# Encoder block on one core: fewer weight planes in front of attention, a third probability buffer, squares on ScalarE alone, first columns over seven buffers

## The chip, the cores and the metric

The kernel runs on one core of a Trainium2 chip. The engines of a core work on their own instruction queues, each in its own order, and wait for one another by semaphores: TensorE (PE, matrix products into PSUM banks), VectorE (DVE), ScalarE (ACT), GpSimd (POOL), and SyncE (SP), which here issues nearly all DMA transfers. The metric is the device time of one execution in microseconds (us); a time is a median of several executions.

## The reference

An encoder block on 1024 tokens of width 1024, batch 1, depth 1:

```python
h = layer_norm(x, ln0_g, ln0_b)
proj = h @ w_in + b_in                       # qa ka va | qb kb vb | ga gb
y_na  = neighbourhood_attention(qa, ka, va, na_rpb) @ w_branch_na     # 8 heads, 16x64 grid
y_swa = windowed_gqa_with_sink(rot(qb), rot(kb), vb, swa_sink) @ w_branch_swa  # 8 heads, window 128
mixed = sigmoid(ga) * y_na + sigmoid(gb) * y_swa
h = layer_norm(2**0.25 * h + mixed @ w_out + b_out, ln1_g, ln1_b)
u = square(relu(h @ w_ff1 + b_ff1))
h = layer_norm(2**0.25 * h + u @ w_ff2 + b_ff2, ln2_g, ln2_b)
```

Everything is float32. The kernel keeps that accuracy by splitting each factor of a product into a high and a low 16-bit plane (or a high and a low rounded 32-bit part in attention) and adding three products: high by high, high by low, low by high.

## The kernel before, in words

**Stages.** First layer norm and transposition of the tokens, with the first two gate chunks' products (0 to about 48 us of the profile); projections in front of attention (to 92); 16 attention heads with the other projections woven between (to about 400); the rest of the gates by a Strassen-like scheme of seven products (to about 500); branch products, output projection and second layer norm; the two feed-forward layers, seven products again, to the end.

**First columns.** `ln0_turn(half, k)` takes transposed column k (128 features) of one half (512 tokens) out of PSUM. ScalarE writes the affine result `t` in float32 (L384), then the high plane is made by ScalarE (L383, for k in `HI_ACT`) or DVE (L386), and the low plane (L387) by GpSimd if k is in `LO_ON[half]`, else by DVE. Three of four groups of `t` are stored to DRAM (`hq_d`, L391), and the buffer of `t` is free again only when that store has landed. `t` borrows buffers that attention uses later: `vt` and `x2` (one each), `pl` (two) and `pt` (three). `PRE_AT` says at which column iteration i a preparation step of chunk 0 or 1 is issued.

**Chunks.** The projection weights come in 24 chunks of 1024x128 (`fills`), numbered j from 0: 0 and 1 are key and value of the windowed attention, 2 its first queries, 3 to 8 more queries and gates, 9 on the neighbourhood attention. Each is prepared in five steps (`Chunk.to`): (1) sum of squares, on ScalarE (L213) or, from `ON_DVE` on, on DVE (L210); (2) a total over partitions by two small PE matmuls (L193); (3) a scale from it, DVE (L199) and GpSimd (L200); (4) the high plane on ScalarE (L252); (5) the low plane on DVE (L254). Raw weights lie in a ring of three places, so chunk j's load waits until chunk j-3's low plane is made. The planes lie in a ring of three pair buffers (`wpair`), except for chunks 3 to 8, which have places of their own (`KEPT`).

**Order of the work.** The order on every engine is written out by hand. A generator (`fill`) issues one chunk matmul (L418) at a time; chunk j's 48 matmuls are numbers 48j to 48j+47. `pump(n)` issues n of them, and lowers the counters of all deferred work (`later`) by n; `flush` issues, in the order of the list, what has come due. `plan` puts the load and the preparation steps of all chunks on that list, ahead of everything else, with due counts relative to 48j: in the change below, `t` holds the counts of steps 1, 2-3, 4 and 5. In front of attention the loop issues 4 matmuls and flushes, 188 in all (`N_PRE`). The work that follows a projection half (24 matmuls) is deferred too: eviction at once (L595, L500 and others), then for rotated queries and keys the shuffle (DVE, L603) and three GpSimd passes (L605 to L607) 4 later, the high parts (ScalarE casts, L651, or L630 and L631 for the key) 22 after that, the low parts (DVE, L656, or L636) 8 later still.

**Attention.** `steps(s, n, ...)` handles a quarter of a head: scores of piece s+2 by PE (L753, L754) with bias and row maximum on DVE (L755), some of the n chunk matmuls, an early flush (preparation steps 1, 4 and 5 are issued only here), `part_l(s + 1)`: low plane of the probabilities on DVE (L786) and the transposing DMA from `pl` to `pt` (L789), `part_e(s + 2)`: exponentials (ScalarE, L774) and their scaled high plane into `pl` (L777), another flush, more chunk matmuls, `part_c(s - 1)`: probabilities by values on PE (L861), and a last flush, in which totals are issued. n is 12 in the first eight heads and 18 in the last eight. An output bank is drained by ScalarE (L867) and, deferred by 14, by DVE (L870). For the neighbourhood heads, L534 evicts a query-key projection, L537 to L539 cast its high parts (ScalarE) and L544 and L545 make its low parts (DVE).

**The gates behind attention.** `g_mm(p, i)` is product i of gate pair p (12 matmuls of four 128-row blocks, L1138), `g_after` takes it out (ScalarE, L1200, or DVE, L1203) and stores it, `g_sums` forms the next weight sums on DVE (L1107), `g_hi` and `g_lo` their planes (L1123, L1127). `g_do` is the product and, for products 1, 6, 5 and 4, its `g_after`. Product 4 accumulates on the bank that product 7's `g_after` reads.

Of the kernel before, what the change touches and what calls it, by code (L numbers as in the profile page):

```python
# [12 lines left out]
F16 = mybir.dt.float16  # L13
# [3 lines left out]
P = 128  # L17
D = 1024
S = 1024
NK = D // P  # L20
# [38 lines left out]
W_TOP = 8192.0  # L59
Q_MIN = 1e-30  # L60
C_LAG = 1
LO_ON = (2, 3, 4, 5), (1, 3, 5)
RS = 3, 3.5, 4.5, 5.5
HI_AT = 1
PRE_AT = {8: (0, 1), 10: (0, 3), 16: (0, 4), 18: (0, 5), 20: (1, 1)}
KEPT = {3: 'whi0', 4: 'wlo0', 5: 'whi1', 6: 'wlo1', 7: 'raw', 8: 'raw'}
ON_DVE = 12
PREP = 5, 6, 7, 8, 8, 9, 10, 12, 13, 14, 15, 16
HI_ACT = (0, 2, 3, 4, 5), ()
ST0=2  # L70
# [22 lines left out]
def encoder_block(ctx, tc, x, w_in, w_br, w_out, w_ff1, w_ff2, par, rows, rpbp,  # L93
# [131 lines left out]
    class Chunk:  # L225
        def __init__(self, kept=None, on_dve=False):
            i = len(chunks) % 3
            self.raw, self.n, self.on_dve = wraw[i], 0, on_dve
            if kept:
                self.pair = wp.tile([P, 2, 8, P], F16, tag=kept, name="wpair", bufs=2 if kept == "raw" else 1)  # L230
            else:
                self.pair = wpair[n_pair[0] % 3]
                n_pair[0] += 1
            chunks.append(self)

# [140 lines left out]
    def ln0_turn(half, k):  # L376
        cs = slice(half * 512, (half + 1) * 512)
        ps = ln_ps[half, k]
        tag = ("vt", "pl", "x2", "pt")[k % 4]
        t = ap.tile([P, 512], F32, tag=tag, name="t", bufs=dict(pl=2, pt=3).get(tag, 1))  # L380
        aff = dict(bias=g0s[:, 8 + k:9 + k], scale=g0s[:, k:k + 1])
        if k in HI_ACT[half]:
            ACT.activation(hT[:, 0, k, cs], ps, AF.Identity, **aff)  # L383
        ACT.activation(t, ps, AF.Identity, **aff)  # L384
        if k not in HI_ACT[half]:
            DVE.tensor_copy(hT[:, 0, k, cs], t)  # L386
        (POOL if k in LO_ON[half] else DVE).tensor_tensor(out=hT[:, 1, k, cs], in0=t, in1=hT[:, 0, k, cs],  # L387
                                               op=ALU.subtract)
        q = f"A{half + 1}{k // 4 + 1}"
        if q in hq_d:  # L390
            nc.sync.dma_start(hq_d[q][:, k % 4], t)  # L391
# [300 lines left out]
    def plan():  # L692

        def to(j, n):
            return lambda: got[j].to(n)
        ev = []
        for j in range(1, len(todo)):
            u = 48 * j
            t = (u - 84, u - 60, u - 40, u - 20) if j > 8 else \
                [24 * j - 32 + x for x in (0, 14, 38, 44)]  # L700
            if j > 8:
                ev.extend((u - 140 + 8 * x, 0, (j, x)) for x in range(4))
            elif j > 2:
                ev.append((max(24 * (j - 3) + 14, 2), 0, (j, None)))
            ev.extend((x, n, j) for x, n in zip(t, (1, 3, 4, 5)))
        for x, n, j in sorted(ev, key=lambda e: e[0]):
            if n == 0:
                defer(x, lambda j=j: fetch(*j))
            else:
                defer(x, to(j, n), pe=n == 3, only=n != 3)  # L710
# [53 lines left out]
    def part_e(s):  # L764
# [7 lines left out]
        for i, (at, n, c0) in enumerate(tiles):  # L772
            p = e[:, at:at + n]
            ACT.activation(p, p, AF.Exp, bias=nm[:, i:i + 1], scale=-1.0,  # L774
                           accum_out=sums_l[o_chunk][:, hh, 2 * t + i:2 * t + i + 1])
        pl = ap.tile([P, 1536], F16, tag="pl", name="pl")
        ACT.activation(pl[:, 0:n_all], e[:, 0:n_all], AF.Copy, bias=0.0, scale=P_SCALE)  # L777
        hd.pairs[t] = e, tiles, n_all, pl

# [130 lines left out]
    with tc.manual_schedule(engines=MANUAL):  # L910
# [324 lines left out]
        def g_do(p, i):  # L1235
            g_mm(p, i)
            if i in (1, 6, 5, 4):
                g_after(p, i)
# [64 lines left out]
        g_do(3, 3)  # L1303
        g_after(3, 3)
        g_lo(3, 4)
        g_sums(1, 6)
        g_hi(1, 6)
        g_do(2, 7)
        g_lo(1, 6)
        g_after(2, 7)  # L1310
        g_sums(0, 6)
        g_hi(0, 6)
        g_do(3, 7)
# [1113 lines left out]
```

## Time and profile before

| | |
|---|---|
| median of 3 runs | 1264.71 us (1263.72 to 1265.9) |
| profiled execution, its own time | 1266.1 us |
| its span, first to last instruction | 1264.3 us |
| mean granted TensorE clock | 0.990 |
| busy share: PE, DVE, ACT, POOL | 97%, 77%, 66%, 27% |
| DMA | 216.83 MB, mean 172 GB/s |

The profile comes from one execution, recorded by the hardware. A row of an order of time is: start, length, engine, line, operation, what it writes and reads, how many instructions are merged in it (x), and in brackets the engine's idle time before it and what ended that. PEld is TensorE's weight load, which overlaps its products. "hT" is the name of one large tile that also holds the raw weights, the weight pairs and small scales of the chunks.

### The profile page before, as it was taken

What the parts mean: (1) busy time and instruction counts of PE and PEld (TensorE: products, weight loads), DVE (VectorE), ACT (ScalarE), POOL (GpSimd) and SP (SyncE); (2) the same over time, 40 slices, a digit from 0 to 9 for tenths busy, and PEclk for the clock granted to TensorE, in tenths of its full rate; (3) what the DMA queues carried; (4) which work ended last, traced back from release to release, by engine and by line L of the source; (5) the groups of instructions that cost most, each with busy time, mean ns of one, the idle gap of its engine ahead of it and who ended that gap; (6) DMA issues with size and microseconds to landing.
All of it is one profiled execution on the core that took longest, in us unless ns stands there. A gap on an engine that the chain in (4) does not pass through costs nothing.

```text
span 1264.3 us, 16965 instructions
## 1 busy us (share of the span) xinstructions
PE 1226.1 (97%) x6024; PEld 673.7 (53%) x6024; DVE 974.5 (77%) x1396; ACT 829.5 (66%) x1329; POOL 346.6 (27%) x352
## 2 busy tenths in 40 slices
PE   7988999899999999999999999999999999999997
PEld 5545665555555446888884444444444444444443
DVE  6667998798797976444778988787767778898888
ACT  7576789787776645432657877877877646434457
POOL 5462231343341001334731013323300001201207
PEclk9998999899999999999999999999999999999999
DMA  8462668677754425555343267766637635363333
GB/s 320 167 201 73 150 160 186 128 165 155 164 139 126 161 83 183 193 174 216 124 160 117 103 199 248 230 237 221 222 132 259 231 133 226 125 254 129 125 108 134
DMA packets 177877, 216.83 MB, mean 172 GB/s; under 512 B 111744, under 2 KB 125312, under 8 KB 171136
## 3 DMA queue, kind: packets, MB, share of 16 engines
q1 hardware_dynamic: 176816, 214.89, 53.8%
q8 instruction: 47, 0.77, 0.3%
q10 hardware_dynamic: 976, 0.87, 0.2%
q14 instruction: 38, 0.31, 0.1%
HBM read 130.69 MB, written 59.33 MB: 150 GB/s over the span
## 4 chain that ended last, share of the span: by engine, by line
PE 72%; DVE 11%; ACT 7%; DMA 4%; issue 4%; POOL 2%; SPq 0%; POOLq 0%; ACTq 0%; DVEq 0%
PE ps_mm L418 12%; PE ps_o L1660 6%; PE ps_t L1660 6%; PE ps_s L2132 6%; PE ps_mm L2132 6%; PE ps_mm L1660 5%; PE ps_t L2132 5%; PE ps_o L2132 5%; PE ps_s L1660 2%; PE ps_o L861 2%; DMA pt<-pl 1%; PE ps_t L410 1%; PE ps_o L410 1%; PE ps_t L409 1%; PE ps_o L409 1%
## 5 line engine op out<-in xcount | busy, mean ns | idle before, releaser
L418 PE MATMUL ps_mm<-hT 128*128 128x512 f16 x960 | 229.8, 383 | 9.5 <-DVE hT L254 4.4
L1660 PEld LDWEIGHTS <-tw 128*128 128x128 f16 x1248 | 122.1, 99 | 145.1 <-issue 1.7
L2132 PEld LDWEIGHTS <-hS 128*128 128x128 f16 x1008 | 98.6, 98 | 118.2
L418 PEld LDWEIGHTS <-hT 128*128 128x128 f16 x960 | 90.9, 100 | 109.4 <-issue 15.9
L774 ACT ACTIVATE ss<-ss,sk 128x384 f32<-128x384 f32 (+1 forms) x128 | 73.9, 579 | 38.0 <-DVE sk L755 37.8
L1660 PE MATMUL ps_t<-hS,tw 128*128 128x512 f16 x384 | 87.9, 379 | 0.0
L1415 POOL TENSOR_TENSOR mx<-sg 128x512 f32<-128x512 f32 x16 | 32.5, 2033 | 142.2 <-DVE sg L1414 142.2
L786 DVE SCALAR_TENSOR_TENSOR pl<-ss,pl 128x640 f16<-128x640 f32 (+1 forms) x64 | 69.0, 1078 | 2.3 <-ACT pl L777 1.8
L418 PE MATMUL ps_mm<-hT,wpair 128*128 128x512 f16 x288 | 70.4, 385 | 0.0
L1850 DVE TENSOR_TENSOR usl<-usl 128x512 f32<-128x512 f32 x64 | 51.4, 803 | 23.6 <-ACT usl L1778 23.4
L1581 POOL TENSOR_TENSOR c<-c 128x2 f32<-128x2 f32 x16 | 15.6, 978 | 194.0 <-DVE c L1580 194.0
L2152 POOL TENSOR_TENSOR acc<-acc,rst 128x512 f32<-128x512 f32 x16 | 30.2, 1886 | 124.0 <-DMA rst<-xr_d 116.1
L777 ACT ACTIVATE pl<-ss 128x640 f16<-128x640 f32 (+1 forms) x64 | 50.6, 790 | 19.1 <-DMA pt<-pl 17.6
L200 POOL TENSOR_TENSOR hT<-hT 128x2 f32<-128x2 f32 x30 | 26.6, 889 | 128.7 <-DVE hT L199 128.7
L1138 PEld LDWEIGHTS <-hT 128*128 128x128 f16 x336 | 33.3, 99 | 43.1 <-issue 5.3
L1965 DVE SCALAR_TENSOR_TENSOR hS<-stg,c,hS 128x2048 f16<-128x2048 f32 x21 | 49.9, 2378 | 7.6 <-ACT hS L1962 7.6
L1587 DVE SCALAR_TENSOR_TENSOR tw<-raw,c,tw 128x512 f16<-128x512 f32 x60 | 51.8, 864 | 4.5 <-ACT tw L1584 4.2
L2132 PEld LDWEIGHTS <-hA 128*128 128x128 f16 x336 | 32.9, 98 | 39.6
L861 PE MATMUL ps_o<-pt,vv 128*128 128x256 f16 (+1 forms) x448 | 49.7, 251 | 3.7 <-DVE oT L870 3.3
L861 PEld LDWEIGHTS <-vv 128*128 128x128 f16 x448 | 35.7, 98 | 21.1 <-DVE oT L870 4.2
L1660 PE MATMUL ps_o<-hS,tw 128*128 128x512 f16 x192 | 44.0, 379 | 0.0
L1584 ACT ACTIVATE tw<-raw,c 128x512 f16<-128x512 f32 x60 | 41.7, 709 | 2.8 <-DVE raw L1625 2.8
(398 smaller groups left out, 3072.0 us busy)
## 6 DMA issues: line engine op xcount, KB each, us to landing
us_d<-usl SPq DMA_DIRECT2D x112, 256.0 KB, 3.0
stg<-us_d SPq DMA_DIRECT2D x28, 1024.0 KB, 4.8
raw<-in_w_ff SPq DMA_DIRECT2D x24, 512.0 KB, 5.4
sg<-sg_d SPq DMA_DIRECT2D x32, 256.0 KB, 3.6
hA<-in_w_ff SPq DMA_DIRECT2D x8, 1024.0 KB, 7.4
hS<-in_w_ff SPq DMA_DIRECT2D x8, 1024.0 KB, 7.8
hT<-in_w_in SPq DMA_DIRECT2D x60, 128.0 KB, 2.6
hT<-in_w_in SPq DMA_DIRECT2D x11, 512.0 KB, 4.4
```

Source lines behind the costliest of these rows:

```text
L418: PE.matmul(ps, a[:, k, :], act(b, k), start=(k == 0 and i == 0), stop=(k == NK - 1 and i == 2))
L774: ACT.activation(p, p, AF.Exp, bias=nm[:, i:i + 1], scale=-1.0, accum_out=sums_l[o_chunk][:, hh, 2 * t + i:2 * t + i + 1])
L777: ACT.activation(pl[:, 0:n_all], e[:, 0:n_all], AF.Copy, bias=0.0, scale=P_SCALE)
L786: DVE.scalar_tensor_tensor(out=pl[:, n:2 * n], in0=e[:, 0:n], scalar=P_SCALE, in1=pl[:, 0:n], op0=ALU.mult, op1=ALU.subtract)
L861: PE.matmul(o, vs, move(part), start=(m == 0 and part == 0), stop=(m == len(runs) - 1 and part == 1))
L1138: PE.matmul(ps, w[:, a, k, :], act[:, b, k, :], start=(first and k == 0 and m == 0), stop=(k == 3 and m == 2), skip_group_check=True)
L1584: ACT.activation(hi_lo(slot, 0), src, AF.Copy, bias=0.0, scale=w_scale(p))
L1587: DVE.scalar_tensor_tensor(out=hi_lo(slot, 1), in0=src, scalar=w_scale(p), in1=hi_lo(slot, 0), op0=ALU.mult, op1=ALU.subtract)
L1660: PE.matmul(ps, ww, act[:, part, k, :], start=(first and k == 0 and m == 0), stop=(k == 3 and m == 2), skip_group_check=True)
L1850: DVE.tensor_tensor(out=out, in0=a, in1=b, op=op)
L1965: DVE.scalar_tensor_tensor(out=slot[:, :, 1, :], in0=src, scalar=scale, in1=slot[:, :, 0, :], op0=ALU.mult, op1=ALU.subtract)
L2132: PE.matmul(ps, st[:, a, part, j * P:(j + 1) * P], w[:, a, wpart, :], start=(first and a == 0 and m == 0), stop=(a == 3 and m == 2), skip_ ...
```

## The change

Six edits:

- `LO_ON`: column 5 of the first half leaves GpSimd; its low plane is made by DVE. `PRE_AT`: chunk 0's total and scale are issued at i = 12 in place of 10. `ln0_turn`: `t` goes round seven buffers in place of the four names in turn.
- `ON_DVE = 99`: the squares of chunks 12 to 23 go from DVE to ScalarE.
- `Chunk`: from the sixth chunk without a place of its own (that is chunk 9) on, the planes take two pair buffers in turn, not three.
- `part_e`: every third `pl` lies in the third pair buffer's place, so that there are three places for probabilities.
- `plan`: chunks 1 to 6 are due every 20 counts in place of 24, chunks 7 and 8 only behind the start of attention (200 to 304); for chunks 9 on, squares are due at u-96 (was u-84), totals at u-72 (u-60), high planes at u-44 (u-40), low planes at u-28 (u-20), loads 10 earlier, with u = 48j.
- the gates: product 7 of pair 2 and its `g_after` come ahead of the sums and the high plane for product 6 of pair 1.

```diff
-LO_ON = (2, 3, 4, 5), (1, 3, 5)
+LO_ON = (2, 3, 4), (1, 3, 5)
-PRE_AT = {8: (0, 1), 10: (0, 3), 16: (0, 4), 18: (0, 5), 20: (1, 1)}
+PRE_AT = {8: (0, 1), 12: (0, 3), 16: (0, 4), 18: (0, 5), 20: (1, 1)}
-ON_DVE = 12
+ON_DVE = 99
@@ class Chunk
-                self.pair = wpair[n_pair[0] % 3]
+                self.pair = wpair[n_pair[0] % 3 if n_pair[0] < 5 else n_pair[0] % 2]
                 n_pair[0] += 1
@@ ln0_turn
-        tag = ("vt", "pl", "x2", "pt")[k % 4]
+        tag = ("vt", "pl", "x2", "pt", "pl", "pt", "pt")[(half * NK + k) % 7]
@@ plan
             u = 48 * j
-            t = (u - 84, u - 60, u - 40, u - 20) if j > 8 else \
-                [24 * j - 32 + x for x in (0, 14, 38, 44)]
+            t = (u - 96, u - 72, u - 44, u - 28) if j > 8 else \
+                [200 + 40 * (j - 7) + x for x in (0, 24, 44, 64)] if j > 6 else \
+                [20 * j - 24 + x for x in (0, 14, 30, 34)]
             if j > 8:
-                ev.extend((u - 140 + 8 * x, 0, (j, x)) for x in range(4))
+                ev.extend((u - 150 + 8 * x, 0, (j, x)) for x in range(4))
             elif j > 2:
-                ev.append((max(24 * (j - 3) + 14, 2), 0, (j, None)))
+                ev.append((max(20 * (j - 3) + 12, 2) + (30 if j > 6 else 0), 0, (j, None)))
             ev.extend((x, n, j) for x, n in zip(t, (1, 3, 4, 5)))
@@ part_e
-        pl = ap.tile([P, 1536], F16, tag="pl", name="pl")
+        pl = ext[:, 10240:11776] if s % 3 == 0 else ap.tile([P, 1536], F16, tag="pl", name="pl")
@@ the gates
         g_lo(3, 4)
+        g_do(2, 7)
+        g_after(2, 7)
         g_sums(1, 6)
         g_hi(1, 6)
-        g_do(2, 7)
         g_lo(1, 6)
-        g_after(2, 7)
         g_sums(0, 6)
         g_hi(0, 6)
         g_do(3, 7)
```

## The prediction

> **What bounds the kernel now.** I read the page first, then TensorE's list of waits, then the order of time of each engine around each wait.
>
> ```profile
> span 1264.3 us, 16965 instructions
> PE 1226.1 (97%) x6024; PEld 673.7 (53%) x6024; DVE 974.5 (77%) x1396; ACT 829.5 (66%) x1329; POOL 346.6 (27%) x352
> PE ps_s L753 <- DVE q L656: 6.7, 1, 6.7
> PE ps_mm L418 <- DVE hT L254: 4.4, 5, 1.9
> PE ps_o L861 <- DVE oT L870: 3.3, 1, 3.3
> PE ps_o L1138 <- DVE go L1203: 2.4, 1, 2.4
> ```
>
> TensorE (PE) is busy 97% of the span, so it sets the end, and what can be won lies in the 38 us in which it isn't. The list (total, times, longest) says where: 6.7 us in one wait for a split query (L656) as attention starts, 4.4 us for late low weight planes (L254), 3.3 us for an output bank to be drained (L870), 2.4 us in the gate products (L1203). A wait can also cost clock. First three waits in order of time (start, length, and in brackets the idle time before), then stretches of time with their length, the busy time of PE, PEld, DVE, ACT and POOL, and PE's granted clock.
>
> ```profile
> 262.14 1.47 PE L418 MATMUL ps_mm<-hT 128*128 128x512 f16 x6 [1.33 <-DVE hT L254]
> 306.45 1.89 PE L418 MATMUL ps_mm<-hT 128*128 128x512 f16 x6 [1.92 <-DVE hT L254]
> 351.03 1.47 PE L418 MATMUL ps_mm<-hT 128*128 128x512 f16 x6 [0.63 <-DVE hT L254]
> ```
>
> ```profile
> 95.73:102.56 6.83, 3.97 (x11) 2.01 (x12) 4.50 (x7) 2.44 (x6) 3.23 (x2) 0.50 0.00 0
> 225.44:232.27 6.83, 6.25 (x22) 3.46 (x23) 5.24 (x11) 5.36 (x13) 1.67 (x2) 0.50 0.80 186
> 262.99:266.40 3.41, 3.41 (x18) 1.90 (x17) 3.38 (x9) 1.62 (x3) 1.86 (x4) 1.00 0.13 30
> 307.36:310.77 3.41, 3.41 (x11) 1.91 (x10) 3.38 (x9) 1.45 (x3) 1.56 (x3) 0.50 0.26 59
> ```
>
> Behind the waits that end at 98.6, 226.0 and 306.5 the clock is 0.5 for 6.8, 6.8 and 3.4 us. Half of what PE worked there is lost: 2.0, 3.1 and 1.7 us. Behind the wait of 1.33 us, which ends at 262.1, the clock stays whole. So a wait of 1.3 us costs itself, and one of 1.9 us cost 3.6. [...]
>
> **First columns, and a squares' total two columns later.**
>
> ```profile
> 22.40 0.78 ACT L384 ACTIVATE t<-ps_s,hT 128x512 f32<-128x512 f32 x1 [1.56 <-DMA hq_dA<-t]
> 22.02 0.27 POOL L349 TENSOR_SCALAR mv<-mv 128x1 f32<-128x1 f32 x1
> 31.46 0.38 PE L193 MATMUL ps_t<-hT 128*128 128x2 f32 x2 [0.71 <-ACT hT L213]
> ```
>
> ScalarE (ACT) waits 1.56 us for a store to free "vt" in column 4; with seven buffers that column has a fresh one. Only part comes through: the normalisation behind it needs GpSimd's scale of 22.02 to 22.29, so it starts 0.7 us earlier than now, and so does ScalarE's unbroken work up to the second half. Column 5's low half goes from GpSimd to DVE (L387), where it stands ahead of the last statistics; GpSimd's scale still comes before its normalisation, so that costs nothing (bound: 0.7, if the normalisation has to wait). The total, moved two columns on, no longer makes PE wait 0.71 us for its square. I take -1.2; bounds -2.3 (1.56+0.71) and 0 (the next column's wait takes it all).
>
> **In front of attention.** Positions are counts of matmuls since the first projection ("at 48"). In one flush the planned plane work runs ahead of evictions queued later, and every engine keeps its order.
>
> ```profile
> 59.15 0.78 ACT L595 ACTIVATE qf<-ps_mm,prm,hT 128x512 f32<-128x512 f32 x1 [2.46 <-PE ps_mm L418]
> 61.00 0.62 ACT L630 CAST kh<-qf 64x512 fp32r<-64x512 f32 x1 [1.07 <-POOL qf L607]
> 64.58 1.04 ACT L213 ACTIVATE hT<-hT 128x1024 fp8e5<-128x1024 f32 x1
> 60.93 0.70 POOL L200 TENSOR_TENSOR hT<-hT 128x2 f32<-128x2 f32 x1
> 79.75 1.28 POOL L605 TENSOR_TENSOR qf<-qf,rt 128x512 f32<-128x512 f32 x1 [2.85 <-DVE hT L199]
> 83.32 1.27 POOL L607 TENSOR_TENSOR qf<-qf,qs 128x512 f32<-128x512 f32 x1
> 59.87 0.33 SPq L238 DMA_DIRECT2D hT<-in_w_in  x1
> 61.34 5.34 PE L418 MATMUL ps_mm<-hT 128*128 128x512 f16 x24
> 89.17 2.75 PE L418 MATMUL ps_mm<-hT,wpair 128*128 128x512 f16 x12
> 78.95 0.73 DVE L603 STREAM_SHUFFLE qs<-qf 128x512 f32<-128x512 f32 x1
> 96.79 2.37 DVE L656 TENSOR_TENSOR q<-qf,q 64x512 fp32r<-64x512 f32 x2
> ```
>
> Now PE arrives at 91.92 (89.17+2.75) and starts at 98.59, 1.8 us after the first L656 began. Ahead of L656 stand the planes of chunks 6 and 7. The change puts chunk 7's behind the start of attention and chunk 6's at 126 to 132, where chunk 5's were. But it packs six chunks where five were, and that makes the queries late.
>
> Chunk 2's high plane moves from 56 to 48, ahead of the eviction at 59.15. Its scale is ready at 61.63 (60.93+0.70), behind the rotation on GpSimd. So ScalarE does the plane (1.15) to 62.8, the eviction (0.78) to 63.4, four casts (0.62 each, at 61.00 now) to 65.9, chunk 4's square with its readout (1.04+0.19, at 64.58 now) to 67.1. PE wants that square's total at 72, that is 61.34+16x0.216 = 64.8 (the row's 24 matmuls start at 56, 0.216 apart): a new wait of 2.3 us, with all products behind it.
>
> ScalarE goes on with plane 3 (68.2), an eviction (68.9), square 5 (70.0), casts (72.5), plane 4 (73.6). Chunk 6 can be fetched only when chunk 3's low plane has left its place, about 69.5; it lands 4.7 us later (as 59.87 to 64.58 now), and its square ends at 75.4. Then the value's eviction 76.2, its maximum on DVE 77.7, its high half and four copies 79.6, plane 5 80.7, the first query eviction 81.4. DVE puts chunk 5's low plane and the value's low half ahead of the query's shuffle: that starts at 83.3, in place of 78.95.
>
> From there the shorter chain runs: shuffle and a rotation with one plane beside it, as now from 79.75 to 84.59 (4.84), to 88.9; second shuffle and rotation to 94.5; DVE's next shuffle to 95.2, with the cast beside it; plus the 1.8: PE starts at 97.0. It arrives at 92.7, so it still waits 4.3 us. I take 97.0-98.59 = -1.6, with the same clock loss behind it. Bounds: if the shuffle keeps its place at 78.95, all ends 4.4 us earlier and PE starts on arrival, without the 2.0 us of clock: -8. If the casts slip further and the new wait halves the clock too (1.7): +3. For that clock I add 0.5, chance about a third.
>
> **Third probability buffer, squares on ScalarE.**
>
> ```profile
> ACT pl L777 <- DMA pt<-pl: 17.6, 16, 2.7
> L210 DVE SCALAR_TENSOR_TENSOR hT<-hT 128x1024 fp8e5<-128x1024 f32 x12 | 15.1, 1261 | 0.0
> L213 ACT ACTIVATE hT<-hT 128x1024 fp8e5<-128x1024 f32 x14 | 14.7, 1050 | 2.3 <-DMA hT<-in_w_in 1.7 <-ACT rt L813 0.5
> L213 ACT ACTIVATION_READ_ACCUMULATOR hT<-hT 128x1 f32 x14 | 2.6, 189 | 0.0
> 176.00:400.00 224.00, 214.91 (x1215) 124.61 (x1214) 191.85 (x384) 175.22 (x349) 73.07 (x87) 0.98 0.68 155
> 218.88 0.84 ACT L777 ACTIVATE pl<-ss 128x768 f16<-128x768 f32 x1 [0.82 <-DMA pt<-pl]
> 220.40 0.90 DVE L544 TENSOR_TENSOR kl<-hT,q 64x512 fp32r<-64x512 f32 x1 [2.78 <-ACT q L537]
> 223.27 1.22 DVE L210 SCALAR_TENSOR_TENSOR hT<-hT 128x1024 fp8e5<-128x1024 f32 x1
> 225.29 0.68 DVE L870 TENSOR_TENSOR oT<-ps_o,oT 64x512 f32<-64x512 f32 x1
> 226.02 1.25 PE L861 MATMUL ps_o<-pt,vv 128*128 128x256 f16 x6 [3.28 <-DVE oT L870]
> ```
>
> Twelve squares of 1.26 us leave DVE and come to ScalarE at 1.05+0.19: 14.9 us. From 176 to 400, ScalarE goes from 175 to 190 busy of 224 us, DVE from 192 to 177. The third buffer takes away ScalarE's 17.6 us of waits for transposes. Where PE doesn't wait, both are worth nothing. It waits from 222.7 to 226.0, for the bank's drain (225.29). That stands behind a square (223.27), which stands behind DVE's wait of 2.78 us for ScalarE's casts, which stand behind the buffer wait of 0.82 us. The change removes the 0.82 and the square. But by the new due counts chunk 12's low plane (a DVE pass of 1.3 us) comes a step earlier, into the square's place. And on ScalarE chunk 12's square comes two steps further ahead (0.9 of its 1.24 reaches the casts, by DVE's waits there) and chunk 13's comes in front of these casts (1.24-0.82 = 0.4; smaller buffer waits before it, which go too, give about that back). So the drain ends 0.9 us later: +0.9. Bounds: -6.4 (3.28 and its 3.1 of clock, all gone) and +2.5 (both squares in full).
>
> **Planes further ahead, two pair buffers.** The waits at 262.1, 306.5 and 351.0 are every third chunk's: with 18 matmuls a step, due at u-20 falls 6 matmuls ahead of use (u) for chunks 14, 17 and 20. Due at u-28 falls 24 ahead for these, and no chunk has fewer than 12; those with 12 now don't wait. So 1.33+1.92+0.63 and the 1.7 of clock go: -5.6. Two buffers in place of three I cost at nothing: chunk j's high plane overwrites the pair last read at u-48 and is due at u-44 or later, and ScalarE's own work of a step hides the difference; without that cover it is four matmuls (0.9 us) for each of some ten chunks. Bounds: -5.6, and -1.6 with 0.4 for each of ten.
>
> **The gates' order.**
>
> ```profile
> 449.96 0.69 DVE L1107 TENSOR_TENSOR graw<-graw 128x512 f32<-128x512 f32 x1
> 453.69 7.03 PE L1138 MATMUL ps_o<-hT 128*128 128x512 f16 x24 [2.42 <-DVE go L1203]
> 456.48 0.74 DVE L1203 SCALAR_TENSOR_TENSOR go<-ps_o,hT,go 128x512 f32<-128x512 f32 x1
> ```
>
> Product (2,4) starts at 453.69, behind L1203 of (2,7), which DVE does after the sums that begin at 449.96. Moved ahead of these, it ends at 450.7, and (2,4) starts 2.4 us earlier, at 451.3. But L1203 of (3,7), at 456.48, stays behind the same DVE work, and (3,4), which follows (2,4), needs it: PE then waits from 453.9 to 457.2. The wait moves by one product, and with it any clock loss: 0; bounds -2.4 (the wait gone) and +1 (3.3 for 2.4).
>
> **Sum:** -1.2-1.6+0.5+0.9-5.6+0 = -7.0. The profiled execution took 1266.1 us with its span of 1264.3, and lies 1.4 above the runs' median of 1264.71. 1266.1-7.0 = 1259.1, less 1.4: 1257.7.
>
> **Rivals.**
> 1. *The front wait goes.* For it: the planes of chunk 7 no longer stand ahead of L656. Against: the late shuffle above. -8 in place of -1.6: 1251.3.
> 2. *The late planes' gain is eaten*, by high planes that wait for two buffers, or by squares that fall into the same step as the plane before (2.4 us together on ScalarE, for two chunks of three). Half a microsecond for each of ten chunks makes the -5.6 a -0.6: 1262.7, no change to be seen. Against it: DVE has 15 us more to catch up.
> 3. *ScalarE becomes the bound* between 176 and 400, and the third buffer doesn't do what it says, since ScalarE waits for scores instead of transposes. Each square then costs PE its 1.24 us. It is slower from the point where more than 7.0/1.24, about 6, of the eleven squares beyond the sum's come through; with nine, 1257.7+11.2 = 1268.9. Against it: 34 of 224 us stay free.
>
> **Chances.** Forecast 0.48, rivals 0.20, 0.16 and 0.16. About 0.2% (2.5 us, so 1262.2 to 1267.2) can't be told from no change. Nearly all of the forecast's own range (1254 to 1262) and rival 1 are faster: 0.69; rival 2 and a little of the others are the same: 0.17; most of rival 3 is slower: 0.14. The predicted time is 1257.7; the range runs from 1246 (rival 1, with most of the bank wait gone too) to 1267 (rival 3 with some seven squares).
>
> **What would show it.** Right: PE's list has no L254 wait of a microsecond between 250 and 360; a wait of about 2 us stands at a squares' total near 65; L753 starts near 96 after about 4 us; the L861 wait stays at 3 to 5; the L1138 wait sits one product later; L777 waits for no transposes. Wrong: no L753 wait (rival 1), waits for L252 or for the L870 drain all through 176 to 400 (rivals 2 and 3).

## The result, and the profile after

| | before | changed |
|---|---|---|
| median of 4 runs | 1265.31 us (1263.72 to 1266.63) | 1255.63 us (1253.18 to 1256.89) |
| profiled execution, its own time | 1266.1 us | 1255.74 us |
| span | 1264.3 us | 1253.9 us |
| mean granted TensorE clock | 0.990 | 0.993 |

The ratio is 0.9922, with a 95% interval of 0.9902 to 0.9941: 9.7 us less, where 7.0 were forecast. One execution of a later experiment (squares back on DVE) took 1582.16 us at a mean granted clock of 0.752, and is left out of that experiment's numbers. In the changed kernel all lines from 701 on are one higher (L753 is L754, L861 is L862, L870 is L871, L1138 is L1139).

The page of the changed kernel (span, busy time) and TensorE's list of waits (total, times, longest):

```profile
span 1253.9 us, 16974 instructions
PE 1222.4 (97%) x6024; PEld 671.9 (54%) x6024; DVE 960.0 (77%) x1373; ACT 841.8 (67%) x1353; POOL 340.3 (27%) x351
PE ps_s L754 <- DVE q L656: 3.9, 1, 3.9
PE ps_o L1139 <- DVE go L1204: 3.4, 1, 3.4
PE ps_t L754 <- DVE sk L756: 3.0, 1, 3.0
PE ps_t L193 <- ACT hT L213: 2.7, 2, 2.2
PE ps_mm L418 <- DVE hT L254: 0.5, 2, 0.3
```

TensorE is still busy 97% and still sets the end. Its waits for low planes (L254) are gone, 4.4 us before and 0.5 now. The wait for the first query has fallen from 6.7 to 3.9, and a wait of 2.2 for a square (L213) has come ahead of it, as forecast. The gates' wait is 3.4 in place of 2.4. The bank wait of 3.3 has changed its name: TensorE now waits 3.0 a few matmuls earlier, for DVE's row maximum. ScalarE's waits for a transposing DMA to free "pl", 17.6 us before, are all gone.

TensorE's order of time at the first three of these waits (start, length, and in brackets the idle time before), then its clock behind them (stretch, its length, busy time of PE, PEld, DVE, ACT, POOL, and the granted clock):

```profile
65.77 0.38 PE L193 MATMUL ps_t<-hT 128*128 128x2 f32 x2 [2.16 <-ACT hT L213]
96.10 0.58 PE L754 MATMUL ps_s<-kh,q 128*128 128x256 f32 x1 [3.86 <-DVE q L656]
222.32 0.58 PE L754 MATMUL ps_t<-kh,q 128*128 128x256 f32 x1 [2.95 <-DVE sk L756]
```

```profile
92.10:95.51 3.41, 0.15 (x1) 0.00 (x0) 0.88 (x3) 1.69 (x3) 2.46 (x3) 1.00 0.00 0
95.51:98.92 3.41, 2.82 (x8) 1.56 (x9) 3.22 (x6) 0.95 (x4) 3.36 (x2) 0.50 0.00 0
98.92:102.34 3.42, 3.42 (x10) 1.35 (x8) 0.00 (x0) 3.06 (x6) 1.27 (x1) 0.50 0.00 0
218.39:221.80 3.41, 0.98 (x5) 0.47 (x3) 2.28 (x5) 2.27 (x5) 3.00 (x6) 1.00 1.25 150
221.80:225.22 3.42, 2.90 (x8) 1.43 (x9) 3.42 (x7) 3.35 (x7) 0.15 (x1) 0.50 0.04 14
443.67:447.08 3.41, 1.08 (x6) 0.49 (x6) 2.56 (x4) 3.30 (x5) 0.00 (x0) 1.00 0.09 34
447.08:450.50 3.42, 3.42 (x10) 1.22 (x9) 1.89 (x2) 0.70 (x2) 0.00 (x0) 0.50 0.98 254
```

Leaving out the last 7 us of each, the clock is half for 13.65 us in all (6.83, 3.41 and 3.41), where before it was half for 20.5 (6.83, 6.83, 3.41 and, in the gates from 454.13 on, 3.41).

Laid side by side by the number of the chunk product (the n-th L418 matmul is the same work in both), the lead of the changed kernel grows and shrinks like this:

| stretch | forecast | measured | what the rows show |
|---|---|---|---|
| first columns, to 48 us | -1.2 | -1.3 | the normalisation (L357) starts at 22.38 in place of 23.08, and the wait of 0.71 at the total is gone |
| to the first scores, at 98.59 and 96.10 | -1.6, with +0.5 for clock | -1.2 | starts near 96 after 3.9 us |
| clock behind them | none beyond that | +1.1 | 6.24 us are worked at half clock, 3.97 before |
| bank drain near 222 | +0.9 | -2.0 | the products on the bank start 1.0 later in this count, but nothing behind them is worked at half clock, where 6.25 us were |
| 240 to 351 us, low planes | -5.6 | -6.2 | all three L254 waits gone |
| 351 to 407 us | 0 | -1.8 | a wait of 1.07 us at 380.99, and a smaller one, gone |
| gates, to 460 us | 0 | +1.0 | 3.43 for 2.42, the wait one product later |

Together that is -10.4, the difference of the two profiled times. The largest forecast came out in sign and size. That isn't yet evidence that its cause is the one that the prediction named; the experiments say otherwise.

### The profile page after: what moved, and what is told of

The parts are those of the page before. It is cut to its first block, busy times and chain, and to the rows that moved or that the text cites. A ratio compares the mean times of both kernels' runs of the same rounds, so it can differ in the third digit from the quotient of the medians.

```text
span 1253.9 us, 16974 instructions
## 1 busy us (share of the span) xinstructions
PE 1222.4 (97%) x6024; PEld 671.9 (54%) x6024; DVE 960.0 (77%) x1373; ACT 841.8 (67%) x1353; POOL 340.3 (27%) x351
## 4 chain that ended last, share of the span: by engine, by line
PE 76%; DVE 11%; ACT 6%; issue 3%; POOL 2%; DMA 2%; POOLq 0%; ACTq 0%; DVEq 0%
PE ps_mm L418 15%; PE ps_o L1661 6%; PE ps_t L1661 6%; PE ps_mm L2133 5%; PE ps_mm L1661 5%; PE ps_s L2133 5%; PE ps_t L2133 5%; PE ps_o L2133 5%; PE ps_s L1661 2%; PE ps_o L862 2%; PE ps_t L408 1%; PE ps_o L408 1%; PE ps_t L410 1%; PE ps_t L409 1%; PE ps_o L410 1%
## 5 line engine op out<-in xcount | busy, mean ns | idle before, releaser
L418 PE MATMUL ps_mm<-hT 128*128 128x512 f16 x960 | 227.5, 381 | 5.4 <-POOL hT L387 2.1
L418 PEld LDWEIGHTS <-hT 128*128 128x128 f16 x960 | 90.9, 100 | 103.7 <-issue 14.0
L418 PE MATMUL ps_mm<-hT,wpair 128*128 128x512 f16 x288 | 71.2, 390 | 0.0
L1139 PEld LDWEIGHTS <-hT 128*128 128x128 f16 x336 | 33.3, 99 | 44.1 <-issue 6.3
L862 PE MATMUL ps_o<-pt,vv 128*128 128x256 f16 (+1 forms) x448 | 49.1, 250 | 0.1
L787 DVE SCALAR_TENSOR_TENSOR pl<-ss,pl 128x768 f16<-128x768 f32 (+1 forms) x42 | 46.5, 1107 | 1.3 <-ACT pl L778 1.1
L862 PEld LDWEIGHTS <-vv 128*128 128x128 f16 x448 | 35.4, 98 | 17.4 <-DVE oT L871 1.8
L418 PEld LDWEIGHTS <-wpair 128*128 128x128 f16 x288 | 27.1, 101 | 29.8 <-issue 5.4
```

Of the source, the lines that this page charges most:

```text
L418: PE.matmul(ps, a[:, k, :], act(b, k), start=(k == 0 and i == 0), stop=(k == NK - 1 and i == 2))
L787: DVE.scalar_tensor_tensor(out=pl[:, n:2 * n], in0=e[:, 0:n], scalar=P_SCALE, in1=pl[:, 0:n], op0=ALU.mult, op1=ALU.subtract)
L862: PE.matmul(o, vs, move(part), start=(m == 0 and part == 0), stop=(m == len(runs) - 1 and part == 1))
L1139: PE.matmul(ps, w[:, a, k, :], act[:, b, k, :], start=(first and k == 0 and m == 0), stop=(k == 3 and m == 2), skip_group_check=True)
```

## The experiments

Each kernel was timed beside the kernel before, on the same chip. Ratios are to the kernel before, with 95% intervals, taken from the runs as they stood side by side, so they can differ by a thousandth from the quotient of two medians. The kernel before had a median of 1264.2 in the first four, 1263.11 in the next four and 1264.71 in the last three, against 1265.31 beside the changed kernel. So a difference of medians from the changed kernel is good to a microsecond or two only; where it matters, the lead by chunk products in the traces is given beside it.

**The front's old schedule.** The changed kernel, with chunks 1 to 8 prepared by the old due counts.

```diff
-                [200 + 40 * (j - 7) + x for x in (0, 24, 44, 64)] if j > 6 else \
-                [20 * j - 24 + x for x in (0, 14, 30, 34)]
+                [24 * j - 32 + x for x in (0, 14, 38, 44)]
...
-                ev.append((max(20 * (j - 3) + 12, 2) + (30 if j > 6 else 0), 0, (j, None)))
+                ev.append((max(24 * (j - 3) + 14, 2), 0, (j, None)))
```

> The changed kernel with the planes in front of attention due as before (every 24 counts, chunks 7 and 8 too). Theory: the new schedule won 1.1 us of start and lost 1.1 us of clock behind it, so undoing it changes little: no wait at the total near 65 us, a wait of about 6.7 us at the first scores, which start near 97.3 us (98.59 less the 1.3 of the first columns), and a time within 1.5 us of the changed kernel's 1255.6. Rival: the new schedule is a main part of the gain, through what it does later in attention; then 1259 or more.

Measured: 1254.36 us (1253.65 to 1258.22), ratio 0.9931 [0.9915, 0.9948], no different from the changed kernel. TensorE's order of time has the long wait back and no wait near 65:

```profile
97.24 0.55 PE L753 MATMUL ps_s<-kh,q 128*128 128x256 f32 x1 [6.66 <-DVE q L656]
```

The new front schedule takes 2.8 us from this wait and gives them back at the square's total and in clock. In itself it is worth nothing that these runs can tell from zero.

**A lighter front.** Here the cadence stays the old one, and chunks 6, 7 and 8 are all put behind the start of attention.

```diff
-                [200 + 40 * (j - 7) + x for x in (0, 24, 44, 64)] if j > 6 else \
-                [20 * j - 24 + x for x in (0, 14, 30, 34)]
+                [200 + 40 * (j - 6) + x for x in (0, 24, 44, 64)] if j > 5 else \
+                [24 * j - 32 + x for x in (0, 14, 38, 44)]
...
-                ev.append((max(20 * (j - 3) + 12, 2) + (30 if j > 6 else 0), 0, (j, None)))
+                ev.append((max(24 * (j - 3) + 14, 2) + (30 if j > 5 else 0), 0, (j, None)))
```

> The changed kernel with the old 24-count cadence for chunks 1 to 5, and chunks 6, 7 and 8 all due behind the start of attention. Theory: the wait at the first scores is left because six planes are packed where five were, which puts the key's eviction behind a high plane on ScalarE. With the old cadence and no plane behind chunk 5's, the first shuffle starts near 78 us, the scores start on TensorE's arrival near 90.5 us with no wait over 1 us, the clock stays whole there, and the wait of 2.2 us at the total near 65 is gone: 8 to 9 us faster than the changed kernel, about 1247, less what one more plane costs in attention. Rival: the rotation on GpSimd alone keeps the query late; then a wait of 3 us or more stays and the gain is under 3 us.

Measured: 1247.79 us (1246.52 to 1249.55), ratio 0.987 [0.9853, 0.9886], 7.8 us under the changed kernel, 8.1 by the traces at the end of attention. TensorE's order of time at the first scores, where no idle time is noted:

```profile
89.34 0.42 PE L754 MATMUL ps_s<-kh,q 128*128 128x256 f32 x1
```

The wait is gone, with its clock (the first score takes 0.42 us, and took 0.58 at half clock in the changed kernel). So planes in front of the query were the cause of it; what kept the change from this gain is that it packed six chunks into the time of five. (This run changes the cadence and the number of chunks together, and doesn't tell their shares apart.)

**Work put into the front wait.** Sixteen 128x512 products that nobody reads are issued ahead of the first scores; all else is computed as in the changed kernel.

```diff
         counts = [CNT[0]] * 8 + [CNT[1]] * 8
+        held = psum("o")
+        for _ in range(16):
+            PE.matmul(held, hT[:, 0, 0, 0:P], hT[:, 0, 0, 0:512], start=True, stop=True)
```

> The changed kernel with 16 more products (128x512, 3.45 us in all, result not read) ahead of the first scores, where TensorE waits 3.86 us. Theory: the wait costs its 3.9 us and, behind it, half of the 6.2 us that are worked at clock 0.5. Filled, the wait is no shorter in time but the clock stays 1.00 behind it: the first scores start where they do now (96.1 us), and the time falls by about 3.1 us. Rival: the lower clock hides behind the other engines there; then no gain.

Measured: 1252.1 us (1251.59 to 1253.93), ratio 0.991 [0.9895, 0.9925]. Scores begin at 97.10, a microsecond later than in the changed kernel. That microsecond isn't the added products': it was lost ahead of them, where ScalarE waited longer for a weight load and began a square (L213) at 75.22 in place of 74.24. The clock behind the wait is whole:

```profile
97.10 0.39 PE L754 MATMUL ps_s<-kh,q 128*128 128x256 f32 x1 [0.42 <-DVE q L656]
96.60:103.40 6.80, 6.38 (x32) 3.46 (x32) 5.58 (x13) 4.29 (x10) 4.55 (x3) 1.00 0.00 0
```

The kernel with more work is 3.5 us faster by the medians, but only 1.5 by the ratios, whose intervals overlap; so the trace decides. It starts the scores 1.0 later than the changed kernel and is 2.0 ahead a dozen chunk products on: 3.0 us of difference, the price of the clock behind this wait by itself (half of the 6.24 us worked there would be 3.1).

**Both gate products ahead of the sums.** Product (3,7) and its take-out are moved ahead of the sums too.

```diff
         g_after(2, 7)
+        g_do(3, 7)
+        g_after(3, 7)
         g_sums(1, 6)
...
         g_hi(0, 6)
-        g_do(3, 7)
         g_lo(0, 6)
-        g_after(3, 7)
```

> The changed kernel with both take-outs of product 7, pairs 2 and 3, ahead of the sums for product 6. Theory: the change only moved the wait from product (2,4) to (3,4), since (3,7)'s take-out stayed behind the sums. With both moved, the waits there (3.43 us) and the 1.7 us of clock behind go: about 4.5 to 5 us faster than the changed kernel, near 1251. Rival: the low planes for product 6, now later, make the next product wait as long; then no gain.

Measured: 1250.6 us (1248.47 to 1252.43), ratio 0.9895 [0.988, 0.991], 5.0 under the changed kernel (3.4 by the ratios, 5.2 in the traces from the first gate product to the end). No wait for a take-out and no half clock are left in the gates (in the changed kernel 3.43 and half of 3.42): the 24 products from 442.97 on take 5.34 us. The change moved one of two products, and so moved the wait.

**Squares back on DVE.**

```diff
-ON_DVE = 99
+ON_DVE = 12
```

> The changed kernel with the squares of chunks 12 to 23 on DVE as before. Theory: squares reach TensorE only near 222 us, where DVE waits for ScalarE's casts (3.04 us before 219.45); on DVE they run in that wait, the casts come 1.2 to 2 us earlier, and TensorE's wait of 2.95 us there falls to between 1 and 1.7, with its clock whole: 1.5 to 3 us faster than the changed kernel. No new wait between 230 and 400. Rival: DVE is the tight engine there (86% busy before), and with the squares back it makes TensorE wait; then slower than the changed kernel by 2 us or more.

Measured: 1253.31 to 1255.56 us in three executions, ratio 0.9924 [0.9905, 0.9943], that of the changed kernel. TensorE's order of time near 222 shows three shorter waits in place of the one of 2.95, and the clock stays whole (six L862 products take 0.71 and 0.72 us, and took 1.25 at half clock in the kernel before):

```profile
218.02 0.71 PE L862 MATMUL ps_o<-pt,vv 128*128 128x256 f16 x6 [0.81 <-DMA pt<-hT]
220.71 0.38 PE L754 MATMUL ps_t<-kh,q 128*128 128x256 f32 x1 [0.63 <-DVE sk L756]
223.90 0.72 PE L862 MATMUL ps_o<-pt,vv 128*128 128x256 f16 x6 [0.94 <-DVE hT L199]
```

By 240 us this kernel leads the changed one by 1.9 us, as expected, and keeps the lead to the end of attention, with no new waits. In the gates the same wait of 3.4 us then costs more than in the changed kernel: the 36 products behind it take 10.63 us from the start of the first to the start of what follows them, in place of 9.45, and 1.2 of the lead are gone. Over the runs nothing remains that they can tell from zero. So the move of the squares is worth little either way: the rival fell, and the theory's gain is there in the trace and not in the times.

**Two places for the probabilities, the rest changed.** This is where the explanation by due counts fell.

```diff
-        pl = ext[:, 10240:11776] if s % 3 == 0 else ap.tile([P, 1536], F16, tag="pl", name="pl")
+        pl = ap.tile([P, 1536], F16, tag="pl", name="pl")
```

> The changed kernel with two places for the probabilities. Theory: ScalarE's waits for transposes (17.6 us before) come back nearly in full, but TensorE sees only those right ahead of 222 us, about 1 us: the wait there grows from 2.95 to about 3.5 to 4.5, and the time by 1 to 3 us (the clock with it). Rival: the third place is what pays for the squares on ScalarE; without it several waits for ScalarE's work appear between 176 and 400 and the time rises by 4 us or more.

Measured: 1264.8 us (1263.43 to 1268.5), ratio 1.0012 [1.0001, 1.0022]. Without the third place the whole gain is lost, with every new due count in force. ScalarE's list of waits, TensorE's order of time, and ScalarE's just ahead of the last of these rows:

```profile
ACT pl L778 <- DMA pt<-pl: 21.3, 15, 2.4
```

```profile
294.09 1.89 PE L418 MATMUL ps_mm<-hT 128*128 128x512 f16 x8 [1.17 <-ACT vf L478]
339.45 1.89 PE L418 MATMUL ps_mm<-hT 128*128 128x512 f16 x8 [2.22 <-ACT vf L478]
```

```profile
337.87 0.74 ACT L778 ACTIVATE pl<-ss 128x640 f16<-128x640 f32 x1 [2.30 <-DMA pt<-pl]
338.63 0.78 ACT L478 ACTIVATE vf<-ps_mm,prm,hT 128x512 f32<-128x512 f32 x1
```

TensorE waits twice for a value's eviction (L478), 1.17 and 2.22 us. Ahead of the second ScalarE waits 2.30 us for a transposing DMA to free "pl". Behind that stands the eviction, and TensorE needs the bank that it empties. TensorE is there some 5.3 us ahead of the kernel before, by its chunk products, and the eviction only 2.0 (338.63 for 340.60): the planes are in time, ScalarE isn't, and the wait comes out at the eviction, not at the plane. The three L254 waits are gone here too, and where they stood 6.2 us are gained, as in the changed kernel; but 5.2 are lost again between them, with these evictions, and 3.0 near 375. The theory (1 to 3 us slower) failed, and the time rose by as much as the rival said; whether the squares on ScalarE are the reason, as it had it, this run doesn't show.

**The old due counts for chunks 9 on.** Three places, two pair buffers.

```diff
-            t = (u - 96, u - 72, u - 44, u - 28) if j > 8 else \
+            t = (u - 84, u - 60, u - 40, u - 20) if j > 8 else \
...
-                ev.extend((u - 150 + 8 * x, 0, (j, x)) for x in range(4))
+                ev.extend((u - 140 + 8 * x, 0, (j, x)) for x in range(4))
```

> The changed kernel with the due counts of chunks 9 to 23 as before (two pair buffers kept). Theory: TensorE's waits for low planes come back at chunks 14, 17 and 20 (1.3, 1.9 and 0.6 us, with 1.7 of clock where it is near 2), and the two totals meet again near 370 us (1.3 to 1.8): 6 to 8 us slower than the changed kernel, about 1262. Rival: the waits at 262, 306 and 351 were lost to DVE's load, which the squares' move lowered; then they stay away and the time is within 2 us of the changed kernel.

Measured: 1251.36 us (1249.98 to 1252.82), ratio 0.9899 [0.9882, 0.9915]. It was to be 6 to 8 us slower than the changed kernel, and is 4.3 faster (2.9 by the ratios). TensorE's order of time:

```profile
219.51 0.72 PE L862 MATMUL ps_o<-pt,vv 128*128 128x256 f16 x6 [1.36 <-DVE oT L871]
252.02 1.47 PE L418 MATMUL ps_mm<-hT 128*128 128x512 f16 x6 [0.73 <-DVE hT L254]
```

One wait for a low plane is left, of 0.73 us. The bank wait is 1.36, and the clock behind it stays whole (1.00 from 219 to 226); there this kernel gains 3.3 us on the changed one. It gives 1.0 back at the low plane, and 1.2 near 366, where a wait of 0.94 for a total's scale (L199) has returned. A lead of 3.0 arises in front, ahead of anything that this edit moves, and is no effect of it. So in the trace the new due counts earned 2.2 us and cost 3.3 near 222, where a square and a plane stand together ahead of ScalarE's casts; with the old counts the square (at 216.19) comes behind the casts (from 214.27). Neither the theory nor the rival (within 2 us) had this.

**Only the totals' old due count.**

```diff
-            t = (u - 96, u - 72, u - 44, u - 28) if j > 8 else \
+            t = (u - 96, u - 60, u - 44, u - 28) if j > 8 else \
```

> The changed kernel with only the totals of chunks 9 to 23 due at u-60 as before. Theory: chunk 23's total falls in the same flush as a gate pair's total again; both hold a bank that the next scores need, and TensorE waits for DVE to read them: one wait of 1 to 1.3 us near 370 us, 1.3 to 1.8 us slower than the changed kernel. Rival: that wait went because DVE has less to do; then no difference.

Measured: 1256.15 us (1255.94 to 1256.69), ratio 0.9936 [0.9919, 0.9953]. TensorE's order of time near 370, where the wait for L199 has come back, at 0.31 and not at 1 to 1.3:

```profile
370.47 0.39 PE L754 MATMUL ps_t<-kh,q 128*128 128x256 f32 x1 [0.31 <-DVE hT L199]
```

Up to 368 us this kernel is level with the changed one (0.2 behind), by 396 it has lost 1.0. So of the 1.8 us gained at 380, which the prediction didn't have, about 1.0 belongs to the totals' due count. How the rest divides isn't settled. By the medians nothing can be told (0.5).

**The third place alone.** The kernel before, with every third "pl" in the third pair buffer's place and, to make room, two pair buffers from chunk 9 on. Nothing else of the change.

```diff
-                self.pair = wpair[n_pair[0] % 3]
+                self.pair = wpair[n_pair[0] % 3 if n_pair[0] < 5 else n_pair[0] % 2]
...
-        pl = ap.tile([P, 1536], F16, tag="pl", name="pl")
+        pl = ext[:, 10240:11776] if s % 3 == 0 else ap.tile([P, 1536], F16, tag="pl", name="pl")
```

> The kernel before with only the third place for the probabilities (and the two pair buffers that make room for it); due counts and squares as before. New theory, since the late planes did not come back with the old due counts and the time rose by 9 us with two places: the lateness at 262, 306 and 351 us began at ScalarE's waits for the transposing DMA, which held up value evictions behind them and through these DVE; the third place alone ends it. Then the L254 waits of 1.3 and 1.9 us go, what is left there is under 1 us each, and the time falls by 6 to 9 us against the kernel before. Rival: it takes the earlier due counts or the squares' move too; then waits of 1 us or more at two of these places stay and the gain is under 3 us.

Measured: 1254.75 us (1253.38 to 1255.39), ratio 0.9921 [0.9904, 0.9937]: 10 us, as much as the whole change. The front wait (6.7) and the gates' stay, and so does the one for L199 near 370 (1.07); the L254 waits go, with the old due counts and with the squares on DVE. By the chunk products 6.1 us are gained from 240 to 356 us, at the three L254 waits, and 4.6 before that, at the bank's drain near 222. There TensorE waits 1.27 in place of 3.28, and the clock behind it stays whole (1.00 from 219 to 230), where 3.1 us were lost:

```profile
224.91 0.72 PE L861 MATMUL ps_o<-pt,vv 128*128 128x256 f16 x6 [1.27 <-DVE oT L870]
```

The chain that led to the first L254 wait, in the kernel before, ScalarE and then DVE:

```profile
251.16 0.74 ACT L777 ACTIVATE pl<-ss 128x640 f16<-128x640 f32 x1 [2.43 <-DMA pt<-pl]
251.93 0.78 ACT L478 ACTIVATE vf<-ps_mm,prm,hT 128x512 f32<-128x512 f32 x1
```

```profile
252.74 1.22 DVE L451 TENSOR_REDUCE mv<-vf 128x1 f32<-128x1024 f32 x1 [3.31 <-ACT vf L478]
260.73 1.35 DVE L254 SCALAR_TENSOR_TENSOR hT<-hT 128x1024 f16<-128x1024 f32 x1
```

and the same instructions in the kernel with the third place:

```profile
244.64 0.74 ACT L777 ACTIVATE pl<-ss 128x640 f16<-128x640 f32 x1
245.41 0.78 ACT L478 ACTIVATE vf<-ps_mm,prm,hT 128x512 f32<-128x512 f32 x1
```

```profile
246.22 1.22 DVE L451 TENSOR_REDUCE mv<-vf 128x1 f32<-128x1024 f32 x1 [0.91 <-ACT vf L478]
254.82 1.28 DVE L254 SCALAR_TENSOR_TENSOR hT<-hT 128x1024 f16<-128x1024 f32 x1
```

ScalarE waits 2.43 us for the DMA that reads "pl". The value's eviction stands behind it. DVE waits 3.31 us for that eviction, and then has the value's maximum (L451), a square and the probabilities ahead of the low plane (L254), which comes at 260.73, so that TensorE waits 1.33. With the third place the wait of 2.43 is gone. By that kernel's chunk products TensorE is already 4.1 us ahead here, from the place near 222; DVE's maximum comes 6.5 us earlier (2.4 beyond that) and the low plane 5.9 (1.8 beyond that), in time for the products, though its due count is the old one. The same four rows stand at 295.01 to 305.04 in the kernel before, ahead of the wait of 1.92 us, and at 339.84 to 349.61, ahead of the one of 0.63.

**What points to a better kernel, joined.** The lighter front, both gate products moved, and the old due counts from chunk 9 on; three places, squares on ScalarE. The edits are those shown above.

> The changed kernel with chunks 6, 7 and 8 due behind the start of attention and the old cadence ahead of it, both take-outs of product 7 ahead of the sums, and the old due counts for chunks 9 on. If the three gains add (8, 5 and 4 us against the changed kernel's 1255.6) it takes about 1239. If the wait near 222 us is only moved by the earlier start, 1242 or more.

Measured: 1240.26 us (1239.85 to 1241.84), ratio 0.9811 [0.9797, 0.9826]. That is 24.4 us under the kernel before and 15.4 under the changed one; the three gains singly (7.8, 5.0, 4.3) add up to 17.1. By the ratios it is 14.0, and 12.9 singly. TensorE's waits between 50 and 500 us that reach a microsecond:

```profile
PE ps_o L862 <- DVE oT L871: 1.3, 1, 1.3
PE ps_t L754 <- DVE hT L199: 1.0, 1, 1.0
```

The wait near 222 us (1.3, at 213.6 here) is no bigger than with the old counts alone (1.36). No half clock is left (1.00 from 30 to 1232) until the last 6 us, in which TensorE has no work.

**Joined, with the squares on DVE.**

> The same with the squares of chunks 12 to 23 on DVE. Theory: with the old due counts a square no longer falls in one step with the plane before it, the wait near 222 us is small either way, and the place of the squares makes less than 2 us. Rival: DVE, with the squares back, drains output banks late near 222 us: a wait of 2 us or more there, and 3 us slower than with the squares on ScalarE.

Measured: 1241.82 us (1241.47 to 1243.4), ratio 0.9824 [0.9809, 0.9838], within 2 us of the one before it. Neither of TensorE's waits at the place near 222 (1.06 and 1.17) reaches the rival's 2. Here it matters little which engine squares.

## Why the prediction was right, and where it was wrong

**The time** came out, 1255.63 for 1257.7, and so did the direction. That the sum fits is in part luck: its largest term has the right size by an edit that without the third place gains nothing and with it isn't needed, and the terms near 222 us (2.9 us better than forecast), near 380 (1.8 better) and of the gates (1.0 worse) miss on both sides. Step by step:

**First columns** (-1.2): -1.3. The size holds, and so do the steps in the trace: the normalisation starts 0.7 us earlier, and the total makes TensorE wait no more. This edit wasn't undone by itself.

**In front of attention** (-1.6). The chain worked out by hand holds. Rows of the changed kernel, ScalarE, then DVE:

```profile
60.32 1.15 ACT L252 ACTIVATE hT<-hT 128x1024 f16<-128x1024 f32 x1 [4.97 <-POOL hT L200]
64.57 1.06 ACT L213 ACTIVATE hT<-hT 128x1024 fp8e5<-128x1024 f32 x1
```

```profile
83.30 0.72 DVE L603 STREAM_SHUFFLE qs<-qf 128x512 f32<-128x512 f32 x1
```

ScalarE makes the plane at 60.32, then squares chunk 4 at 64.57 (64.58 before, though the products come 1.35 us earlier), and TensorE waits 2.16 for the total (2.3 forecast). The shuffle begins at 83.30 (83.3) and the scores at 96.10 after 3.86 us (near 96, about 4). TensorE's arrival, 92.7 in the prediction's count, is given there without a working; with the 1.33 us of the first columns put back it was 93.57. What failed is "with the same clock loss behind it": 1.1 us more of it. The new wait cost no clock in this profile; in that of the kernel with both gate products moved it did (below).

**Third place and squares, the 222 us place** (+0.9): -2.0. The order of the work is as forecast, the size and the sign aren't. ScalarE, then DVE, then TensorE, in the changed kernel:

```profile
214.53 1.05 ACT L213 ACTIVATE hT<-hT 128x1024 fp8e5<-128x1024 f32 x1
215.57 1.14 ACT L252 ACTIVATE hT<-hT 128x1024 f16<-128x1024 f32 x1
```

```profile
219.45 0.76 DVE L544 TENSOR_TENSOR kl<-hT,q 64x512 fp32r<-64x512 f32 x1 [3.04 <-ACT q L537]
224.25 0.67 DVE L871 TENSOR_TENSOR oT<-ps_o,oT 64x512 f32<-64x512 f32 x1
```

```profile
222.92 3.04 PE L418 MATMUL ps_mm<-hT 128*128 128x512 f16 x8
```

Chunk 13's square and chunk 12's plane stand ahead of the casts, and DVE waits 3.04 us for these (2.78 before). The drain ends at 224.92, 225.97 before: of the 1.2 us that the kernel had in hand there, less than 0.2 is used up, not 0.9. The products on the bank start at 225.79, 226.02 before, and so lose 1.0; the rest of that is clock, since the eight products ahead of them take 3.04 us at half clock, where the same eight took 1.90. Behind them the clock is whole again, and the 3.1 us that were lost there aren't lost now. The term let the clock stay as it was, and that turned its sign. It also lumped edits that pull apart: the third place alone gains 4.6 us here, and with the squares and the new counts 2.0 are left.

"Where PE doesn't wait, both are worth nothing" is the sentence that failed. It held for the squares (no new wait outside this place with them on either engine). For the third place it looked only at whether TensorE waits for the engine with the buffer wait; but that wait was the head of a chain that ended in the L254 waits, an engine and nine microseconds further on.

**Planes further ahead** (-5.6). The size came out (-6.2), the cause only in part. The prediction put the three waits down to due counts, since chunks 14, 17 and 20 had only 6 matmuls of room. With the new counts and two places the three waits do go, as it said, but TensorE waits elsewhere and the gain is nil. With the old counts and the third place one wait of 0.73 is left of them, and with the third place alone all of the gain is there (6.1). So the counts needed the third place to pay, and with it they weren't needed. By these runs chunks with little room were those that a late DVE hit first. The earlier counts by themselves, with two places and the squares on DVE, weren't run. That two pair buffers cost nothing holds: the third place alone has them too, and between 235 and 400 us TensorE's only wait there of over 0.2 us is the one for L199.

**The gates** (0; bound +1): +1.0. The wait moved by one product, as worked out, and grew by the bound that was given.

**Not foreseen**: 1.8 us near 380. There the product that opens a piece of scores stood behind a scale that came late for a total, and the totals' new due count moved it (about 1.0 of the 1.8, by the run with the old one); the prediction read only waits of L254 for the effect of the counts.

Of the rivals, the first (no front wait) didn't come, and the lighter front shows that it was to be had. The second was in part right about the wrong place: squares and planes in one step do cost, near 222. The third fell: ScalarE, with 12 more squares and three places, is no bound.

## What to carry to other kernels

When a planned piece of work is late on an engine, follow that engine's own idle time back to its head before giving the piece an earlier due count: here the head was a wait for a buffer, on another engine and nine microseconds earlier, and one more buffer alone gave 10 us, as much as the whole change, while the rest of the change without that buffer, earlier counts included, gave none. An engine's buffer wait can't be called free because TensorE isn't waiting for that engine; what stands behind it in the same queue (an eviction, and who waits for that) is what it costs. And where a change is made of several edits, a sum that comes out proves none of its terms: the third place alone, and the rest without it, told what the total couldn't.

## What the runs showed of the hardware that was not expected

**The same wait cost clock in some profiles and none in others.** Stretches of the kernel before about its waits of 3.28, 1.33 and 1.92 us (which end at 226.02, 262.14 and 306.45), then of the kernel with both gate products moved and of the changed kernel about the same wait near 65 us:

```profile
222.03:225.44 3.41, 0.71 (x4) 0.10 (x1) 3.38 (x9) 2.53 (x6) 0.86 (x2) 1.00 0.02 5
225.44:228.85 3.41, 2.83 (x13) 1.81 (x13) 3.41 (x7) 2.24 (x7) 0.00 (x0) 0.50 0.67 147
228.85:232.27 3.42, 3.42 (x11) 1.65 (x11) 1.83 (x5) 3.12 (x7) 1.67 (x2) 0.50 0.93 225
259.57:262.99 3.42, 2.09 (x17) 1.33 (x15) 3.36 (x8) 3.34 (x7) 3.42 (x5) 1.00 0.37 119
303.95:307.36 3.41, 1.49 (x14) 0.92 (x12) 3.35 (x8) 2.82 (x7) 1.36 (x3) 1.00 0.47 136
```

```profile
63.10:66.52 3.42, 1.27 (x8) 0.53 (x7) 3.35 (x4) 3.36 (x6) 3.42 (x3) 1.00 0.93 322
66.52:69.93 3.41, 3.41 (x10) 1.21 (x9) 3.34 (x4) 2.27 (x5) 1.70 (x2) 0.50 0.99 399
```

```profile
61.38:64.79 3.41, 2.23 (x11) 0.79 (x9) 3.26 (x6) 3.33 (x7) 1.86 (x2) 1.00 1.04 386
64.79:68.20 3.41, 2.43 (x13) 1.25 (x14) 3.34 (x3) 3.41 (x5) 3.33 (x3) 1.00 1.00 383
```

Behind the wait of 3.28 us the clock is half for 6.83 us (225.44 to 232.27). Behind that of 1.33 it stays whole, and behind that of 1.92 it is half for 3.41; the rows for these two are in the prediction. The wait near 65 is 2.16 us in the changed kernel and 2.15 in the other, which is the same kernel up to there. In the first TensorE is busy 2.23 and 2.43 us in the two rows, the clock stays whole, and the 20 products behind the wait take 4.48 us. In the second it is busy 1.27 us in the first row, the next is worked at half clock, and the same 20 products take 6.16.

It is so elsewhere too. With the old due counts the wait near 65 is 2.16 again, and the 20 products take 6.16. At the first scores that kernel waits 3.02 us and the twelve chunk products behind them take 2.76, where the one with both gate products moved waits 3.01 and they take 4.45. Near 222 the latter waits 2.50, and eight products behind take 1.90; the changed kernel waits 2.95, and they take 3.04. So the length of such a wait alone doesn't tell its price. Of the waits measured here, those of 1.27 us (the third place alone), 1.33 (the kernel before) and 1.36 (the old due counts) cost no clock, those named from 2.15 to 3.02 cost none or up to 1.7 us, and those of 3.28 (the kernel before) and 3.86 (the changed kernel) 3.1 us each. For this kernel a forecast can give the clock's price of a wait of 2 to 3 us only as a range.

**More work was faster.** Sixteen unread products in a wait that lies on the path won 3.0 us in the trace, since the work behind it ran at whole clock (1.00 from 96.60 to 103.40; the row is shown with that experiment).
